# Two mixture-of-experts layers: the first experts' rows from a one-hot product, the overflow loop at the last pair, the memory keys among the output projection

## The chip, the cores and the metric

The kernel runs on one core of one Trainium2 chip. A time is the device time of one execution, in microseconds (us). The kernel before was timed three times: 2768.33, 2773.16 and 2774.87 us, median 2773.16. A further execution was taken with the hardware profiler: 2772.39 us on the device, of which the profile's span (first to last instruction) is 2770.2 us.

The engines are named as in the profile: PE is TensorE (matrix products), PEld its weight loads, DVE is VectorE, ACT is ScalarE, POOL is GpSimd, SP is SyncE, which here issues nearly all DMAs, in order.

## The reference: two mixture layers, then two dense ones

512 tokens of width 1024 pass through two "first blocks" and two "second blocks". A first block is a mixer and then a mixture of experts; a second block is attention, cross attention to a memory of 256 rows, and a dense feed-forward part. What the change touches:

```
for l in range(2):                                   # first blocks
    y = concat(mLSTM, latent attention, spatial gating)(rms_norm(x, attn_norm[l]))
    x = x + y @ w_out[l]
    xt = rms_norm(x, ffn_norm[l])                    # (512, 1024)
    g  = top1(xt @ w_group[l] + b_group)             # 4 groups
    e  = top2 of the 8 experts of group g            # 32 experts, weights softmaxed
    for each expert: rows = its tokens
        h = silu(xt[rows] @ w1[e]) * (xt[rows] @ w3[e])      # 1024 -> 256
        x[rows] += (h @ w2[e]) * weight                      # 256 -> 1024
for i in range(2):                                   # second blocks
    ...
    k, v = split(rms_norm(mem, mem_kv_g[i]) @ x_wkv[i])      # (256, 2048)
    x = x + cross_attention(x, k, v); ...
```

All products are wanted in float32. The kernel makes most of them from two rounded halves of each operand (`mm3`: high*high, high*low, low*high in fp32r, three passes); the experts' products are plain fp32.

## The kernel before

**The planner.** Every operation is first recorded (`Recorder.add`), then `flush` puts them in order: it prices each (`price`: engine time and, for a DMA, a transfer time in one modelled queue), walks a modelled clock, and on each engine picks among the next 24 ready ones the one with the lowest rank (program place less the length of the path behind it). Tiles come from a heap of 46 buffers of 512 KB and 6 half-size ones. The resulting order per engine is fixed; at run time every engine goes through its own list strictly in order. SP's list is a queue in the same sense: a store that waits for its data holds back the loads behind it.

**f1 (L1397 on)** is a mixer layer. Its last piece, `do_out`, multiplies the four token tiles with `w_out` in two column halves; the second half ends tile by tile in `chain_route` (L1897): transposes of x, the split into high and low, the router's product (L1917), and the normalized rows `xn`, which are stored to DRAM as `xm` (L1923).

**route (L1927)** is a chain of some 110 small DVE operations on the router's result, with one product of counts in its middle; it yields `s.sl` (each token's slot) and `s.ovi` (how many blocks of 64 rows do not fit the fixed capacity of 64 rows per expert).

**mem_kv (L1002)** makes the memory's keys and values for the second block `l`: normalize 256 rows, transpose, 8 key chunks (192 products of 256 columns), 4 value tiles (96 products of 512 columns), all stored to DRAM. It stands in the program behind `route`.

**overflow (L2062)** is a hardware loop over `ovi[0]` blocks. With these inputs the count is zero in both layers: no instruction of its body shows in the trace. The loop is recorded as one operation on all engines ("ALL"): each engine reads the count, stops until every engine has come and the DMAs issued are done, and goes on. It stands before the experts.

**moe (L2163 on)** runs 16 pairs of experts. `prep_group` builds one-hot matrices and from them the row numbers of four pairs; `prep_pair` gathers a pair's 128 rows from DRAM with an indirect DMA on POOL's queue and transposes them (8 transposes); `up` is 32 products of 256 columns in fp32 (two experts side by side in the array's columns; the profile shows 64 records), `down` 8 products of 512, `combine` adds two pairs back to the tokens with 32 products of 512. Each pair's weights are 12 loads of 512 KB (`raw<-w`), 192 loads per layer.

```
G.memset(x, 0.0)                    # two gather buffers, L2171 on
prep_group(0); prep_pair(0)
for p in range(NP + 1):
    up(p, w13)
    prep_pair(p + 1)                # gather, then transposes
    down(p - 1); combine every second pair
```

In `run` (L2287 on) a layer is `f1`, `route`, `mem_kv`, the loads of two pairs, `overflow`, `moe`.

Of the kernel before, what the change touches and what calls it, by code (L numbers as in the profile page):

```python
# [85 lines left out]
class Recorder:  # L86
# [127 lines left out]
    @staticmethod  # L214
    def price(eng, method, outs, ins, k):

        def free(x):
            n = 1
            for v in x.shape[1:]:
                n *= int(v)  # L220
            return n
        if eng == "ALL":
            return 2500, 0
        n = max(free(x) for x in outs + ins) if method != "matmul" else free(outs[0])
        if eng == "PE":
# [6 lines left out]
        psum = any(x.tensor.space == PSUM for x in ins)  # L232
        if eng == "SP" or "dma" in method:
# [241 lines left out]
class Kern:  # L475
# [526 lines left out]
    def mem_kv(s, i):  # L1002

        nc = s.nc
        W = s.I["x_wkv_2"][i]
        kd = s.dr.tile([D, 256], F32, name=f"memk{i}")
        vd = s.dr.tile([256, D], F32, name=f"memv{i}")
        g = s.gain(s.I["mem_kv_g_2"][i])
        mT = s.newXT(256)
        for t in range(2):  # L1010
            m = s.H(name="mem")
            nc.sync.dma_start(m, s.I["mem_2"][0, t * 128:(t + 1) * 128, :])
            xn = s.norm(m, g)
            s.to_T(t, xn, mT)
        for cb in range(2):
            def ck(c, ps):
                o = s.T2()
                nc.scalar.copy(o[:, 0:256], ps[:, 0:256])
                r = (cb * 4 + c) * 128
                nc.sync.dma_start(kd[r:r + 128, :], o[:, 0:256])  # L1020
            s.lin_T(mT, 8, W, cb * 512, 128, 4, ck)
        for cb in range(2):
            w = s.wload(W, 0, 8, D + cb * 512, 512)
            for t in range(2):
                ps = s.PS()
                for k in range(8):
                    s.mm3(ps, mT.get(k, t * 128, t * 128 + 128), w[k], k == 0, k == 7)
                o = s.T2()
                nc.scalar.copy(o, ps)
                nc.sync.dma_start(vd[t * 128:(t + 1) * 128, cb * 512:(cb + 1) * 512], o)  # L1030
        return kd, vd

    def cross(s, i, act, kv, nxt):
        nc = s.nc
# [359 lines left out]
                        streams.remove(x)  # L1394
                        break

    def f1(s, l, act, nxt, xsrc):  # L1397
        nc, I = s.nc, s.I
        xT = act.xT
        W = I["w_in"][l]  # L1400
# [164 lines left out]
        def do_mla():  # L1565
            yield from s.mla(b1, done, doneh)
# [3 lines left out]
        def do_out():  # L1570
            tail = None
            for hf in range(2):
# [3 lines left out]
                for t in range(NT):  # L1576
# [24 lines left out]
                        A.copy(y, ps)  # L1601
                    yield

        def seq(*fs):
# [292 lines left out]
    def chain_route(s, l):  # L1897

        c = Chain(None, None)

        def prep():
            s.moe_start(l)
            s.rg = s.gain(s.I["ffn_norm"][l])

        def f(t):
            nc = s.nc
            if c.act is None:
                c.act = s.newXT()
            xT, x = c.act, s.x[t]
            s.to_T(t, x, xT)  # L1910
            r, v, xn = s.SM(1, "rt_r"), s.SM(1, "rt_v"), s.H(name="xn")
            s.stat(x, r, v)
            ps = s.PS()
            for k in range(8):
                hl = xT.get(k, t * 128, t * 128 + 128)
# [7 lines left out]
            nc.sync.dma_start(s.xm[t * 128:(t + 1) * 128, :], xn)  # L1923
        c.prep, c.call = prep, f
        return c

# [236 lines left out]
    def moe(s, l, raws, nxt):  # L2163
# [4 lines left out]
        mm = nc.tensor.matmul  # L2168
        xe, info, w2, us = {}, {}, {}, {}
        s.nc.AGE = 1000  # L2170
        xring = [s.H(name="xg") for _ in range(2)]  # L2171
        for x in xring:
            G.memset(x, 0.0)
        xring = s.ring(xring, D)
        NP = 16

        def prep_group(g):
            slg = s.SM(8, "slg", 2)
# [11 lines left out]
                    mm(ps[:, pr * 6:(pr + 1) * 6], P[k][:, pr * 128:(pr + 1) * 128], s.rec[:, k * 6:(k + 1) * 6], start=k == 0, stop=k == 7)  # L2190
            info[g] = s.slots(ps[:, 0:24], 4, 128, "sl")

        def prep_pair(p):
            g, i = divmod(p, 4)
            xg = xring()
            s.gather(nc, s.xm, xg, info[g][3][:, i:i + 1])
            x = s.H(name="xe")
            for a in range(2):
                tp = s.TP()
# [67 lines left out]

        if isinstance(nxt, Chain):
            nxt.prep()
        prep_group(0)  # L2270
        prep_pair(0)
        for p in range(NP + 1):
            if p < NP:
                w13, w2[p] = raws.pop(0) if raws else s.pair_raw(l, p)
                up(p, w13)
            if p + 1 < NP:
                prep_pair(p + 1)
                if p % 4 == 1 and p < 12:
# [8 lines left out]
    def run(s):  # L2287
# [40 lines left out]
```

## Time and profile before

| | us or share |
|---|---|
| profiled execution | 2772.39 |
| its span | 2770.2 |
| PE busy | 2675.2 (97%) |
| PEld busy | 2150.9 (78%) |
| DVE busy | 1523.6 (55%) |
| ACT busy | 1169.9 (42%) |
| POOL busy | 632.6 (23%) |
| DMA moved | 421.92 MB |

In the trace the first layer's experts run from about 346 to 615 us, the second layer's from about 948 to 1216. [...] A "record" is one line of the trace; an fp32 product has two of them. In the view by windows a row reads: the stretch, its length, then busy us and instructions of PE, PEld, DVE, ACT and POOL, PE's clock, the DMA engines' busy share, GB/s. In a timeline: start, us, engine, line, operation, tile written and tiles read, size, instructions, in brackets the idle time before and what ended it. In the waits view a row reads: engine, tile and line that waited, what it waited for, us in total, number of waits, the longest.

### The profile page before, as it was taken

What the parts mean: (1) busy time and instruction counts of PE and PEld (TensorE: products, weight loads), DVE (VectorE), ACT (ScalarE), POOL (GpSimd) and SP (SyncE); (2) the same over time, 40 slices, a digit from 0 to 9 for tenths busy, and PEclk for the clock granted to TensorE, in tenths of its full rate; (3) what the DMA queues carried; (4) which work ended last, traced back from release to release, by engine and by line L of the source; (5) the groups of instructions that cost most, each with busy time, mean ns of one, the idle gap of its engine ahead of it and who ended that gap; (6) DMA issues with size and microseconds to landing.
All of it is one profiled execution on the core that took longest, in us unless ns stands there. A gap on an engine that the chain in (4) does not pass through costs nothing.

```text
span 2770.2 us, 40611 instructions
## 1 busy us (share of the span) xinstructions
PE 2675.2 (97%) x15112; PEld 2150.9 (78%) x15112; DVE 1523.6 (55%) x3275; ACT 1169.9 (42%) x2406; POOL 632.6 (23%) x752
## 2 busy tenths in 40 slices
PE   8999799999999899999999999999999999999998
PEld 7878756559888666568788988888888879888887
DVE  6696534346796344363689553344548885542433
ACT  5555211125555011154697442233346764432331
POOL 1613100003523000012454111001325541110012
PEclk9999899999999999999999999999999999999999
DMA  6124899962135999940124322233311233322321
GB/s 178 30 77 161 307 406 370 401 204 81 37 104 198 352 392 389 391 151 28 37 68 145 99 92 73 88 107 106 111 59 51 65 125 101 95 80 78 116 91 47
DMA packets 224056, 421.92 MB, mean 152 GB/s; under 512 B 46064, under 2 KB 112368, under 8 KB 223856
## 3 DMA queue, kind: packets, MB, share of 16 engines
q1 hardware_dynamic: 219248, 410.89, 42.7%
q0 software_dynamic: 4608, 8.40, 0.8%
q8 instruction: 121, 1.98, 0.3%
q14 instruction: 79, 0.65, 0.1%
HBM read 410.83 MB, written 16.78 MB: 154 GB/s over the span
## 4 chain that ended last, share of the span: by engine, by line
PE 81%; DVE 8%; ACT 3%; DMA 3%; issue 3%; POOL 1%; SPq 0%; POOLq 0%; DVEq 0%; ACTq 0%
PE mm L385 75%; PE tp L385 6%; DVE wl L385 2%; DMA xg<-xm,slidx 2%; DVE t L385 1%; ACT t L385 1%; DVE x L385 1%; DMA raw<-w 1%; ACT wh L385 1%; ACT qh L385 0%; DVE nm L385 0%; DMA raw<-x_wkv 0%; DVE xtl L385 0%; DVE pt L385 0%; SPq L385 0%
## 5 line engine op out<-in xcount | busy, mean ns | idle before, releaser
L385 PE MATMUL mm<-wh,xth 128*128 128x512 f32 (+3 forms) x1088 | 403.5, 396 | 0.5 <-ACT xth L385 0.5
L385 PE MATMUL mm<-wl,xth 128*128 128x512 f32 (+3 forms) x1088 | 400.7, 393 | 1.1 <-DVE wl L385 1.0
L385 PE MATMUL mm<-wh,xtl 128*128 128x512 f32 (+3 forms) x1088 | 400.9, 393 | 0.2 <-DVE xtl L385 0.2
L385 DVE SCALAR_TENSOR_TENSOR wl<-raw,pre_g,wh 128x512 fp32r<-128x512 f32 (+4 forms) x400 | 286.3, 755 | 151.6 <-ACT wh L385 121.5
L385 PE MATMUL mm<-xth,wh 128*128 128x512 f32 (+1 forms) x1184 | 364.8, 359 | 0.1
L385 PE MATMUL mm<-xth,wl 128*128 128x512 f32 (+1 forms) x1184 | 364.5, 358 | 0.0
L385 PE MATMUL mm<-xtl,wh 128*128 128x512 f32 (+1 forms) x1184 | 363.4, 357 | 0.0
L385 ACT ACTIVATE wh<-raw,pre_g 128x512 fp32r<-128x512 f32 (+4 forms) x400 | 252.0, 685 | 67.9 <-DMA raw<-w_gate_up 50.8
L385 PEld LDWEIGHTS mm<-xtl,wh 128*128 128x128 f32 x1184 | 219.7, 190 | 31.1
L385 PEld LDWEIGHTS mm<-xth,wl 128*128 128x128 f32 x1184 | 219.4, 190 | 30.9
L385 PEld LDWEIGHTS mm<-xth,wh 128*128 128x128 f32 x1184 | 219.2, 190 | 31.1 <-ACT xth L385 0.3
L385 PE MATMUL mm<-raw,xe 128*64 128x256 f32 x2048 | 234.8, 385 | 0.0
L385 PEld LDWEIGHTS mm<-wl,xth 128*128 128x128 f32 x1088 | 204.5, 189 | 35.0 <-DVE wl L385 2.4
L385 PEld LDWEIGHTS mm<-wh,xth 128*128 128x128 f32 x1088 | 204.1, 188 | 35.3 <-ACT xth L385 2.2
L385 PEld LDWEIGHTS mm<-wh,xtl 128*128 128x128 f32 x1088 | 204.8, 188 | 33.6 <-DVE xtl L385 0.7
L385 PEld LDWEIGHTS mm<-raw,xe 128*64 128x64 f32 x2048 | 145.1, 138 | 84.4 <-issue 11.0
L385 POOL TENSOR_TENSOR ffl<-t,ffh 128x512 fp32r<-128x512 f32 x44 | 60.3, 1371 | 544.0 <-ACT ffh L385 506.3
L385 DVE TENSOR_TENSOR wl<-raw,wh 128x1024 fp32r<-128x1024 f32 x112 | 142.1, 1274 | 48.3 <-ACT wh L385 41.2
L385 ACT CAST wh<-raw 128x1024 fp32r<-128x1024 f32 (+2 forms) x128 | 120.4, 956 | 35.1 <-DMA raw<-w_down 30.7
L385 PE MATMUL mm<-raw,t 128*64 128x512 f32 x512 | 125.1, 634 | 7.0 <-ACT t L385 6.9
L385 PE MATMUL mm<-wh,ffh 128*128 128x512 f32 x352 | 130.1, 389 | 0.0
L385 PE MATMUL mm<-wh,ffl 128*128 128x512 f32 x352 | 129.1, 390 | 0.0
(338 smaller groups left out, 4822.6 us busy)
## 6 DMA issues: line engine op xcount, KB each, us to landing
raw<-w SPq DMA_DIRECT2D x384, 512.0 KB, 9.5
raw<-w_gate_up SPq DMA_DIRECT2D x176, 256.0 KB, 3.3
raw<-w_down SPq DMA_DIRECT2D x40, 512.0 KB, 3.8
raw<-x_wkv SPq DMA_DIRECT2D x32, 512.0 KB, 7.3
raw<-a_w_in SPq DMA_DIRECT2D x24, 512.0 KB, 4.0
raw<-b_w_in SPq DMA_DIRECT2D x24, 512.0 KB, 4.1
raw<-w_in SPq DMA_DIRECT2D x24, 384.0 KB, 3.3
raw<-w_out SPq DMA_DIRECT2D x16, 512.0 KB, 3.9
```

Of the source, the lines that this page charges most:

```text
L385: r = o.fn(*o.a, **o.k)
```

## The change

Five edits:

1. **Keys among the mixer.** `mem_kv` now returns two functions. `keys` (normalization, transposes, 8 key chunks) becomes a fifth stream of `f1`, started once five of the eight head results are done; `values` runs after `route`.
2. **Router in smaller tiles.** `chain_route` holds the transposed x per token tile (`TokXT`), so the four splits of 256 columns per engine and tile become two of 512. The tiles `xn` are kept in SBUF.
3. **First pair by a product.** `first_pair` builds, per token tile, the one-hot of slots 0 to 127 (two DVE operations of 128 columns) and multiplies it with `xn`: 32 fp32 products with 128 columns, whose stationary side takes every eighth column of `xn`. Pair 0 has no gather and no transposes any more. Gathers of later pairs are issued two pairs ahead (`fetch`) into three buffers in place of two.
4. **Overflow at the last pair.** The loop is recorded when the last pair's loads have been and before its `up`.
5. **Prices.** A DMA is planned at 400 or 310 (by contiguous bytes) in place of 360, an indirect DMA's delay at 4500 ns in place of 1710; groups are prepared one pair earlier.

```diff
-            return (1040, 1710) if eng == "POOL" else (475, 1100), int(b.shape[0]) * free(b) * DSIZE[b.dtype] / 360
+            return (1040, 4500 if "indirect" in method else 1710) if eng == "POOL" else (475, 1100), int(b.shape[0]) * free(b) * DSIZE[b.dtype] / s_rate(outs + ins)
...
+        def do_beside():
+            while len(doneh) < 5:
+                yield
+            yield from beside()
+
-        s.merge(seq(do_b1, do_csg)); s.merge(seq(do_prep), seq(do_v, do_mo, do_q, do_k, do_mlstm), do_mla(), do_out())
+        s.merge(seq(do_b1, do_csg)); s.merge(seq(do_prep), seq(do_v, do_mo, do_q, do_k, do_mlstm), do_mla(), do_out(), do_beside())
...
-                c.act = s.newXT()
+                c.act = TokXT()
             xT, x = c.act, s.x[t]
-            s.to_T(t, x, xT)
+            xT.add(s)
+            for q in range(2):
+                tp = s.TP()
+                for i in range(4):
+                    nc.tensor.transpose(tp[:, i * 128:(i + 1) * 128], x[:, (4 * q + i) * 128:(4 * q + i + 1) * 128], s.ident)
+                s.split(tp, xT.h[t][:, q * 512:(q + 1) * 512], xT.l[t][:, q * 512:(q + 1) * 512])
...
+        def first_pair():
+
+            oh = s.T2()
+            for t in range(NT):
+                o = oh[:, t * 128:(t + 1) * 128]
+                V.tensor_scalar(o, s.iota[:, 0:128], s.sl[:, t * 2:t * 2 + 1], None, op0=ALU.is_equal)
+                V.scalar_tensor_tensor(o, s.iota[:, 0:128], s.sl[:, t * 2 + 1:t * 2 + 2], o, op0=ALU.is_equal, op1=ALU.add)
+            x = s.H(name="xe")
+            for a in range(2):
+                ps = s.PS()
+                for j in range(4):
+                    for t in range(NT):
+                        mm(ps[:, j * 128:(j + 1) * 128], s.xn[t][:, a * 4 + j:D:8], oh[:, t * 128:(t + 1) * 128], start=t == 0, stop=t == NT - 1)
+                (A.copy if a else V.tensor_copy)(x[:, a * 512:(a + 1) * 512], ps)
+            xe[0] = x
...
+        first_pair()
+        xring = [s.H(name="xg") for _ in range(3)]
...
         prep_group(0)
-        prep_pair(0)
+        fetch(1)
         for p in range(NP + 1):
             if p < NP:
                 w13, w2[p] = raws.pop(0) if raws else s.pair_raw(l, p)
+                if p == NP - 1:
+                    s.overflow(l)
                 up(p, w13)
+            if p + 2 < NP:
+                fetch(p + 2)
...
-            s.f1(l, c.act, s.chain_route(l), I["x"][0] if l == 0 else s.xd)
+            m, keys, values = s.mem_kv(l)
+            kv.append(m)
+            s.f1(l, c.act, s.chain_route(l), I["x"][0] if l == 0 else s.xd, keys)
             s.route()
-            kv.append(s.mem_kv(l))
+            values()
             raws = [s.pair_raw(l, p) for p in range(2)]
-            s.overflow(l)
```

How the order moves at three places of the first layer. (Every recorded operation has the recorder's line, L385 before and L395 now.)

PE before, from the end of the overflow loop on: the last two products of `prep_group` (`tp<-rt_rec,P`), the transposes of gathered rows (`tp<-const,xg`), the first pairs' `up` (`mm<-raw,xe`).

```order
L2076 REGISTER_ALU
L2076 COMPARE_AND_BRANCH
L2076 UNCONDITIONAL_BRANCH
L385 LDWEIGHTS P
L385 MATMUL tp<-rt_rec,P 128x6
...
L385 MATMUL tp<-const,xg 128x128 x13
L385 MATMUL mm<-raw,xe 64x256 x16
```

PE now, up to the first `up`: `mm<-t,xn` is the one-hot product, the rows with 512 columns are the memory's values.

```order
L395 MATMUL tp<-t_717,const 128x32 x14
...
L395 MATMUL mm<-t_781,xn 128x128 x4
...
L395 MATMUL mm<-t_781,xn 128x128 x26
L395 MATMUL mm<-wh,xth 128x512
L395 MATMUL mm<-wl,xth 128x512 x2
...
L395 MATMUL mm<-wl,xth 128x512
L395 MATMUL mm<-raw,xe 64x256 x32
```

The loop is gone from in front of the experts, nothing gathered is used by pair 0, and 96 value products that all stood ahead of the loop are now spread: 16 ahead of the one-hot product and within its start, 14 between it and the first `up`, the rest behind that, 32 of them ahead of the first transposes of gathered rows.

PE before at the last two pairs: `tp<-const,t` and `mm<-raw,t` are a pair's `down`.

```order
L385 MATMUL tp<-const,t_1189 128x128 x2
L385 MATMUL mm<-raw,t_1189 64x512 x8
L385 MATMUL mm<-raw,xe 64x256 x32
L385 MATMUL tp<-const,t_1220 128x128 x2
L385 MATMUL mm<-raw,t_1220 64x512 x8
L385 MATMUL mm<-yh,pT 128x512
```

And now:

```order
L395 MATMUL tp<-const,t_1173 128x128 x2
L395 MATMUL mm<-raw,t_1173 64x512 x8
L395 MATMUL mm<-raw,xe 64x256 x19
L2105 TENSOR_LOAD rt_ovi
L2106 COMPARE_AND_BRANCH
L2106 UNCONDITIONAL_BRANCH x2
...
L2106 REGISTER_ALU
...
L395 MATMUL mm<-raw,xe 64x256 x13
L395 MATMUL tp<-const,t_1222 128x128 x2
L395 MATMUL mm<-raw,t_1222 64x512 x8
```

The loop's stop now stands inside the last pair's `up`, after 19 of its 32 products (after 27 in the second layer).

SP before, in front of the loop and behind it: `memk` and `memv` are stores of keys and values, `raw<-w` experts' weights, `raw<-w_in` the next layer's.

```order
L385 DMA raw<-w 128x1024 x11
L385 DMA memk_665<-t_719 128x256
...
L385 DMA memv_666<-t_753 128x512
L2075 TENSOR_LOAD rt_ovi
...
L385 DMA memv_666<-t_755 128x512
L2076 COMPARE_AND_BRANCH
...
L385 DMA raw<-w 128x1024 x168
L385 DMA raw<-w_in 128x2x416
```

And now:

```order
L395 DMA raw<-w 128x1024 x7
L2105 TENSOR_LOAD rt_ovi
...
L395 DMA memv_117<-t_737 128x512
L395 DMA raw<-w 128x1024 x5
L395 DMA memv_117<-t_739 128x512
...
L395 DMA memv_117<-t_755 128x512
L395 DMA raw<-w 128x1024 x153
L395 DMA raw<-w_in 128x2x416
...
L2106 COMPARE_AND_BRANCH
```

The loads of weights are no longer cut by the loop; the four stores of values now stand among the 24th to 40th load, and of the next layer's weights one load stands ahead of the loop (three in the second layer) where all eight and more did.

## Rows read from the trace of the kernel before

**Rows 1.** By windows: layer 0's router, layer 0's experts, layer 1's router.
```profile
262.00:278.30 16.30, 13.80 (x96) 12.17 (x96) 13.69 (x24) 12.42 (x23) 6.94 (x5) 1.00 0.88 293
...
361.40:480.00 118.60, 117.97 (x864) 73.26 (x863) 52.47 (x113) 22.01 (x41) 9.29 (x10) 1.00 0.99 385
...
868.70:884.70 16.00, 13.51 (x94) 11.92 (x94) 13.34 (x24) 12.13 (x23) 6.62 (x5) 1.00 0.88 298
```
**Rows 2.** Waits of PE from 330 to 350, layer 0.
```profile
PE tp L385 <- DMA xg<-xm,slidx: 7.4, 1, 7.4
PE tp L385 <- issue: 7.0, 1, 7.0
```
**Rows 3.** Waits of PE from 936 to 960, layer 1.
```profile
PE tp L385 <- DMA xg<-xm,slidx: 6.9, 1, 6.9
PE tp L385 <- issue: 4.3, 1, 4.3
```
**Rows 4.** Timeline at the loop, layer 0.
```profile
329.01 1.46 POOL L385 DMA_INDIRECT xg<-xm,slidx  x1 [12.49 <-DVE P L385]
...
336.57 0.21 PE L385 MATMUL tp<-rt_rec,P 128*128 128x6 bf16 x2 [6.96 <-issue]
...
345.95 1.33 PE L385 MATMUL tp<-const,xg 128*128 128x128 f32 x5 [7.36 <-DMA xg<-xm,slidx]
```
**Rows 5.** Chain of work that ended last: start, us, what.
```profile
276.88 19.84 PE mm L385 x164
...
347.28 5.50 PE mm L385 x32
...
361.46 3.60 PE mm L385 x32
...
949.03 5.01 PE mm L385 x32
```
**Rows 6.** Timeline of PE: four fp32 products of 128 columns; eight transposes of gathered rows.
```profile
219.04 1.05 PE L385 MATMUL mm<-qkm 96*128 96x128 f32 x8
...
502.75 1.13 PE L385 MATMUL tp<-const,xg 128*128 128x128 f32 x8
```
**Rows 7.** Weight loads, 20 to 640: count, busy us, mean ns, idle.
```profile
L385 PEld LDWEIGHTS tp<-const,xg 128*128 128x128 f32 x128 | 16.8, 196 | 13.9 <-DMA xg<-xm,slidx 7.8 <-issue 4.0 <-PE mm L385 1.3
...
L385 PEld LDWEIGHTS tp<-const,x 128*128 128x128 f32 x64 | 8.1, 140 | 3.2 <-DVE x L385 1.8
```
**Rows 8.** Timeline of DVE in the routing, layer 0.
```profile
279.83 1.80 DVE L385 TENSOR_TENSOR rt<-rt 128x16 f32<-128x16 f32 x1
...
281.84 1.22 DVE L385 TENSOR_TENSOR wl<-raw,wh 128x1024 fp32r<-128x1024 f32 x1
...
295.68 0.29 DVE L385 TENSOR_TENSOR t<-t 128x128 f32<-128x128 f32 x1
```
**Rows 9.** Timeline of PE at the end of layer 0's experts.
```profile
571.85 0.51 PE L385 MATMUL tp<-const,t 128*128 128x128 f32 x2 [1.48 <-DMA raw<-w]
572.82 5.35 PE L385 MATMUL mm<-raw,t 128*64 128x512 f32 x16 [0.46 <-ACT t L385]
...
594.04 3.65 PE L385 MATMUL mm<-raw,t 128*64 128x512 f32 x16 [0.46 <-ACT t L385]
```
**Rows 10.** Gathers, 320 to 640: time from issue to landing.
```profile
DMA to landing us min/median/max: 6.5/7.6/9.6
```
**Rows 11.** Timeline of SP's queue, layer 0.
```profile
318.00 11.93 SPq L385 DMA_DIRECT2D memv<-t  x4
336.16 231.13 SPq L385 DMA_DIRECT2D raw<-w  x168
568.69 0.38 SPq L385 DMA_DIRECT2D raw<-w_in  x1
```
**Rows 12.** DVE, 560 to 640: splits of the next layer's first weights.
```profile
L385 DVE SCALAR_TENSOR_TENSOR wl<-raw,pre_g,wh 128x416 fp32r<-128x416 f32 x8 | 4.9, 645 | 1.6 <-ACT wh L385 1.6
```
**Rows 13.** Waits of PE, whole span.
```profile
PE tp L385 <- DMA raw<-w: 1.9, 3, 1.5
```

More of the change, by code (lines that the diff above doesn't have):

```diff
@@ L232, in price, with s_rate @@
         psum = any(x.tensor.space == PSUM for x in ins)
+        def s_rate(aps):
+            x = next(v for v in aps if v.tensor.space == bass.MemoryType.DRAM)
+            n = 1
+            for st, c in reversed(list(x.ap)):
+                if st != n and c > 1:
+                    break
+                n *= c
+            return 400 if n * 4 >= 2048 else 310
         if eng == "SP" or "dma" in method:
             b = outs[0] if outs[0].tensor.space != bass.MemoryType.DRAM else ins[0]
-            return (1040, 1710) if eng == "POOL" else (475, 1100), int(b.shape[0]) * free(b) * DSIZE[b.dtype] / 360
+            return (1040, 4500 if "indirect" in method else 1710) if eng == "POOL" else (475, 1100), int(b.shape[0]) * free(b) * DSIZE[b.dtype] / s_rate(outs + ins)
         small = sum(isinstance(x, bass.AP) for x in (k.get("scale"), k.get("bias"), k.get("accum_out")))
@@ L1007, in mem_kv, with keys, ck, values @@
         vd = s.dr.tile([256, D], F32, name=f"memv{i}")
[L1008 to L1023, printed above, removed]
-            for t in range(2):
[L1025 to L1031, printed above, removed]
+        made = []
+        def keys():
+            g = s.gain(s.I["mem_kv_g_2"][i])
+            mT = s.newXT(256)
+            made.append(mT)
+            for t in range(2):
+                m = s.H(name="mem")
+                nc.sync.dma_start(m, s.I["mem_2"][0, t * 128:(t + 1) * 128, :])
+                xn = s.norm(m, g)
+                s.to_T(t, xn, mT)
+                yield
+            for cb in range(2):
+                def ck(c, ps):
+                    o = s.T2()
+                    nc.scalar.copy(o[:, 0:256], ps[:, 0:256])
+                    r = (cb * 4 + c) * 128
+                    nc.sync.dma_start(kd[r:r + 128, :], o[:, 0:256])
+                yield from s.lin_T_steps(mT, 8, W, cb * 512, 128, 4, ck)
+        def values():
+            mT = made[0]
+            for cb in range(2):
+                w = s.wload(W, 0, 8, D + cb * 512, 512)
+                for t in range(2):
+                    ps = s.PS()
+                    for k in range(8):
+                        s.mm3(ps, mT.get(k, t * 128, t * 128 + 128), w[k], k == 0, k == 7)
+                    o = s.T2()
+                    nc.scalar.copy(o, ps)
+                    nc.sync.dma_start(vd[t * 128:(t + 1) * 128, cb * 512:(cb + 1) * 512], o)
+        return (kd, vd), keys, values
     def cross(s, i, act, kv, nxt):
@@ L1395, in merge, with f1 @@
                         break
-    def f1(s, l, act, nxt, xsrc):
+    def f1(s, l, act, nxt, xsrc, beside):
         nc, I = s.nc, s.I
@@ L1602, in do_out @@
                     yield
+        def do_beside():
+            while len(doneh) < 5:
+                yield
+            yield from beside()
         def seq(*fs):
@@ L1902, in prep @@
             s.moe_start(l)
+            s.xn = []
             s.rg = s.gain(s.I["ffn_norm"][l])
@@ L1923, in f @@
             nc.sync.dma_start(s.xm[t * 128:(t + 1) * 128, :], xn)
+            s.xn.append(xn)
         c.prep, c.call = prep, f
@@ L2170, in moe @@
         s.nc.AGE = 1000
[L2171 to L2174, printed above, removed]
         NP = 16
+        xgs = {}
         def prep_group(g):
@@ L2191, in prep_group, with fetch @@
             info[g] = s.slots(ps[:, 0:24], 4, 128, "sl")
+        def first_pair():
[6 more added lines that the diff above has]
+            for a in range(2):
+                ps = s.PS()
+                for j in range(4):
[3 more added lines that the diff above has]
+            xe[0] = x
+        def fetch(p):
+            g, i = divmod(p, 4)
+            xgs[p] = xring()
+            s.gather(nc, s.xm, xgs[p], info[g][3][:, i:i + 1])
         def prep_pair(p):
-            g, i = divmod(p, 4)
-            xg = xring()
-            s.gather(nc, s.xm, xg, info[g][3][:, i:i + 1])
+            xg = xgs.pop(p)
             x = s.H(name="xe")
@@ L2269, in moe @@
             nxt.prep()
+        first_pair()
+        xring = [s.H(name="xg") for _ in range(3)]
+        for x in xring:
+            G.memset(x, 0.0)
+        xring = s.ring(xring, D)
         prep_group(0)
-        prep_pair(0)
+        fetch(1)
         for p in range(NP + 1):
@@ L2274, in moe @@
                 w13, w2[p] = raws.pop(0) if raws else s.pair_raw(l, p)
+                if p == NP - 1:
+                    s.overflow(l)
                 up(p, w13)
+            if p + 2 < NP:
+                fetch(p + 2)
             if p + 1 < NP:
                 prep_pair(p + 1)
-                if p % 4 == 1 and p < 12:
+                if p % 4 == 0 and p < 12:
                     prep_group(p // 4 + 1)
```

## The prediction

> **What bounds the kernel now.** I read first how busy each engine is by stretches, then PE's waits in the two stretches where it is not full, then the timeline around them, and last the queue that feeds the experts. The reader is to see this. In the middle of the first layer's experts PE is busy 117.97 of 118.60 us at full clock, and the DMA engines are busy 0.99 of the time: two resources are nearly full together [rows 1]. PE is the one that leads: in the whole program it waits only 1.9 us for a weight [rows 13], and the 168 loads behind the loop need 231.13 us, so the last is away at 567.3 while PE works on pairs 14 and 15 [rows 9, 11]. So what counts is PE's idle time and PE's own work. Idle time at the start of the experts: 7.0 + 7.4 us in layer 0 [rows 2], 4.3 + 6.9 us in layer 1 [rows 3]. The first of the two is the loop: the gather of pair 0 is issued at 329.01, it takes at least 6.5 us to land [rows 10], that is to 335.5, and PE goes on at 336.57 [rows 4], about 1.1 us later; no engine passes the loop with a gather on its way. The second is the gather of pair 1, whose transposes stand in front of pair 0's `up` on PE: PE stands 7.36 us and goes on at 345.95 [rows 4]. In the routers PE idles 2.5 us each (16.30 less 13.80, 16.00 less 13.51) [rows 1].
>
> **What is removed (layer 0 / layer 1).**
> (a) The two waits, 14.4 / 11.2 us [rows 2, 3]: with the loop gone from there and pair 0 made by a product, neither has a place.
> (b) The slow clock behind them. After these pauses the first 32 records of `up` take 5.50 and 5.01 us, where they take 3.60 later [rows 5]; that is 1.9 / 1.4, and I add 0.6 for transposes of which five took 1.33 us [rows 4] where eight take 1.13 [rows 6]. 2.5 / 2.0.
> (c) The routers' 2.5 us of idle time each fall to about 1.0, since keys and two splits of 512 in place of four of 256 fill or shorten it: 1.6 / 1.6. Bounds 0 and 2.5.
> Sum 18.5 / 14.8.
>
> **What is added.**
> (d) The first pair: 32 fp32 products of 128 columns. Four of these (8 records) took 1.05 us with the pipe's run-out [rows 6]; 32 are at most 8.4. Without the run-out the floor is near that of a pair's 64 `up` records, 7.2 (twice 3.60) [rows 5]. I take 7.5. The eight transposes of pair 0 go, 1.13 [rows 6]: net 6.4 in each layer. The upper bound comes from the stationary side. It takes every eighth column, as the transposes of gathered rows do, and such a weight load took 196 ns against 140 for whole columns [rows 7]; 64 loads of 196 are 12.5 if they set the pace, net 11.4. Against that speaks that eight such transposes still took 1.13 us, 0.14 each, so these loads ran beside the products [rows 6].
> [...]
> (e) New waits in front of the experts, where `values` alone is left as cover. The routing chain on DVE ran from 279.83 to 295.97, but eight splits of the key weights up to 1.22 long stood in it [rows 8]; without them some 6.3 to 7 us. Behind the last router product there are now 62 key products of 0.121 us (164 in 19.84 [rows 5]) and three of values, about twice that each: 8.2 in all. Hidden but for the delay with which the counts' product comes: 0.8. Behind it, the one-hots with 13 value products (3.1 us) as cover: 1.0. Then pair 1's gather: issue 1.46 [rows 4] and half a us for its row numbers, landing 7.6 [rows 10], 9.6, against 32 value products (7.7) and some 1.0 of `prep_group` products: 0.9. Sum 2.7 in each layer, bounds 0 (all is covered) and 6 (nothing is late but each link is doubled). Of pair 0's rows only SBUF tiles are used, so its stores to DRAM delay nothing but the gather of pair 1. The stores of values now stand among the 24th to 40th load on SP and hold the later ones until they are computed; with two pairs of weights loaded PE reaches the third a pair and a half later, so I price this at nothing.
> (f) The loop in the last pair. No gather is under way there, so it drains quickly: the 1.1 us from above plus half a us for the small loads, 1.6; bounds 1.1 and 7.0 [rows 2, 4]. Behind a pause of 1.48 us the next `down` took 5.35 in place of 3.65 us [rows 9]: 1.7 more. 3.3 in each layer.
> (g) In layer 0 one of the pauses between the last `up` products and their `down` (1.48 + 0.46 [rows 9]) is now filled by a combination: −1.9 / 0.
> (h) Queued behind the loop is the next layer's work: on SP all but one load of its first weights (three in layer 1), which started at 568.69 before [rows 11], and on DVE and ACT their splits; eight take 4.9 us on DVE [rows 12]. PE still has 13 (5) products, a `down` and the last combinations to do, which hide most. I take 1.0 each; bounds 0 and 4.9.
> Sum 11.5 / 13.4.
>
> Everything else, the new prices' order of loads included, I put at nothing: in the middle of the experts PE idles 0.6 of 118.6 us [rows 1], so there is nothing to win there, and the weights keep their lead.
> Together: 33.3 less 24.9 is 8.4 us. The profiled execution took 2772.4 us (2.2 more than its span, which I leave as it is) and is 0.8 below the median of the three runs, too little to correct for: 2764.
>
> **The rivals.**
> Strided loads set the pace: 12.5 in place of 7.5 us for the first pair, 10 us more in both layers, 2774, no change. For it rows 7, against it rows 6.
> The late loop costs as much as the early one (slower): it drains 7.0 us [rows 2] in place of 1.6 since loads of the next layer are just under way, and the whole 4.9 of splits [rows 12] then stands in front of the next mixer in place of 1.0. That is 9.3 in each layer, 18.6 in all, 2782.6. It decides from 7.0 us more in each layer (8.4 + 5.5 over two). For it: PE waited 7.0 for whatever was on its way. Against it: no gather is on its way now.
> The DMA engines set the pace after all: then what the loop cost is the pause of the weight stream from 318.00 to 336.16 [rows 11], 18.2 us, and it comes back whole in each layer, 36.4 less the new loop's 6.6: 2742.6. For it: 0.99 busy in the experts [rows 1]. [...] Against it: 1.9 us of waits for weights [rows 13], and a last load some 30 us ahead of its `down`.
>
> **Chances.** Forecast 0.50 (2755 to 2770 by its own bounds), strided loads 0.16, the late loop 0.18, DMA 0.16. A measurement tells a change from none at about 0.2%, 5.5 us. Faster: 0.40 of the forecast's 0.50 and the DMA's 0.16, 0.56. Same: the forecast's other 0.10, 0.12 of the strided loads, 0.02 of the late loop: 0.24. Slower: 0.04 and 0.16, 0.20. The range 2745 to 2782 leaves out the far half of the DMA case and about half of the late loop's.
>
> **What would show it.** (a) No wait of PE for `xg` or "issue" in front of the experts, and (b) the first `up` records at 3.60. (c) Router stretches with about 1 us idle. (d) `mm<-t,xn` summing to 7.2 to 8.4 us, not 12. (e) PE waiting for the counts or `oh` 1 us each, not 3. (f) A pause of PE of 1 to 2 us within the last `up`. (h) The first products of the next mixer waiting for `wl` or `wh` at most 1 us more. The forecast is wrong if PE waits for `raw<-w` early in the experts, or if the second layer's waits are not removed as the first's are.

## The result, and the profile after

The changed kernel takes 2807.59 us, median of four runs (2798.51 to 2809.4), against 2772.29 before: slower, by a ratio of 1.0122, 95% interval [1.0097, 1.0147]. The forecast was 2764 and the range ended at 2782. The profiled execution is the fastest of the four (2798.51, span 2796.7, clock 0.989 where the others show 0.985 to 0.987; a clock is PE's granted one, as a share of its full one), so the traces account for 26 of the 35 us. PE is busy 2705.3 us now, 30 more than before; its idle time in the span is 91, where it was 95. In the traces the loss lies wholly in the two mixture layers: the first ends its last `down` at 623.6 us in place of 612.4, the second 615.9 us after that in place of 599.9, and the rest takes 1557 us in place of 1558.

What the change was to remove is mostly gone. PE's waits over the whole span (engine, tile, line, what it waited for: us, count, longest):

```profile
PE tp L395 <- DVE t L395: 12.0, 10, 2.2
...
PE tp L395 <- DMA xg<-xm,slidx: 6.2, 2, 3.4
PE mm L395 <- ACT t L395: 5.9, 12, 1.1
PE mm L395 <- DVE wl L395: 5.6, 5, 2.1
...
PE tp L395 <- POOL sgo L395: 3.9, 4, 1.5
...
PE mm L395 <- issue: 2.1, 1, 2.1
```

In front of the experts PE stood 14.4 and 11.2 us [rows 2, 3]; of that one wait for gathered rows a layer is left, 6.2 us in all, and it stands behind the first `up` now. The late loop stops PE 2.1 us in layer 0 ("mm <- issue"). New are waits inside the mixer (`sgo` here, `qkm` below). The waits for `t` from DVE and ACT are the largest that the fence shows, 17.9 us together; they are the pauses in the experts' later pairs. They are not new, only left over: the kernel before has nearly the same two.

```profile
PE tp L385 <- DVE t L385: 10.0, 13, 1.5
PE mm L385 <- ACT t L385: 6.9, 15, 0.5
```

So of PE's idle time some 25 us went in front of the experts, and came back as 11 us in the mixers and 10 in the experts (the late gather and the loop). Its busy time rose by 30, and the one new group of products alone is 30.7 in both layers.

The new PE work is that group. Here it is in layer 0, the weight loads first, then the products (count, busy us, mean ns, idle):

```profile
L395 PEld LDWEIGHTS mm<-t,xn 128*128 128x128 f32 x64 | 15.5, 334 | 0.1
```
```profile
L395 PE MATMUL mm<-t,xn 128*128 128x128 f32 x64 | 15.4, 396 | 0.0
```

Loads and products are busy for the same time, 0.24 us a record. Each load takes 334 ns, so one load overlaps the next: 64 of them end to end would be 21.4 us. A strided load of a transpose took 196 ns [rows 7]. That the loads set the pace is shown by the first experiment below (7.6 us of products with loads of 192 ns).

The first `up` behind it runs at full clock (1.00 from 342.8 to 350.2 us), 64 records in 7.13 us, where the first 32 alone took 5.50 [rows 5], at a clock of 0.65 (timeline of PE: start, us):

```profile
343.07 7.13 PE L395 MATMUL mm<-raw,xe 128*64 128x256 f32 x64
```

The mixer of layer 0, from the transposes of `b` on, by windows (length; busy of PE, PEld, DVE, ACT, POOL; clock; DMA; GB/s). Before, its first part and its output projection with the router:

```profile
128.72:200.17 71.45, 69.34 (x400) 57.15 (x400) 64.93 (x159) 33.14 (x80) 11.66 (x13) 0.95 0.23 68
200.17:296.56 96.39, 93.89 (x615) 82.90 (x615) 69.87 (x164) 54.55 (x103) 32.15 (x25) 1.00 0.56 189
```

And after, between the same instructions:

```profile
130.72:203.83 73.11, 68.10 (x368) 56.87 (x367) 65.40 (x155) 37.34 (x87) 11.72 (x13) 0.91 0.25 85
203.83:315.74 111.91, 106.53 (x689) 93.29 (x690) 69.27 (x158) 50.42 (x91) 31.12 (x25) 0.98 0.47 154
```

The second stretch holds all 192 key products now, where 153 stood in it before, so its length doesn't compare; PE's idle time does (length less busy, both stretches together): 4.6 us before, 10.4 after, with a lower clock in both stretches (0.91 and 0.98, where it was 0.95 and 1.00). DVE is busy 91% of the first one in the kernel before already; that is where the keys' norm and splits were added.

The end of layer 1's experts (timeline of PE, in brackets the pause before and what ended it):

```profile
1160.98 0.50 PE L395 MATMUL tp<-const,t 128*128 128x128 f32 x2 [1.42 <-DVE t L395]
1161.94 5.35 PE L395 MATMUL mm<-raw,t 128*64 128x512 f32 x16 [0.46 <-ACT t L395]
...
1195.24 0.47 PE L395 MATMUL tp<-const,t 128*128 128x128 f32 x2 [1.56 <-DVE t L395]
...
1229.14 1.51 PE L395 MATMUL mm<-raw,xe 128*64 128x256 f32 x10 [2.10 <-DVE wl L395]
1232.86 0.51 PE L395 MATMUL tp<-const,t 128*128 128x128 f32 x2 [2.20 <-DVE t L395]
1234.44 5.11 PE L395 MATMUL mm<-raw,t 128*64 128x512 f32 x16 [1.07 <-ACT t L395]
```

At these three places a pair's `down` stands right behind its own `up`, and PE waits for DVE and ACT to make `t` (1.42 and 0.46 us, 1.56 and 0.46, 2.20 and 1.07). The `down` behind them runs at a lower granted clock (0.68, 0.68 and 0.71) and takes 5.35, 5.35 and 5.11 us in place of 3.65 [rows 9]. The pause of 2.10 at 1229 is the loop; the waiter's label names what came last. The clock did not fall behind every such pause: in layer 0 it was 1.00 behind one of 1.56 us (the last line is that layer's loop and the `up` behind it, at 0.65):

```profile
582.18 0.48 PE L395 MATMUL tp<-const,t 128*128 128x128 f32 x2 [1.56 <-DVE t L395]
583.12 3.65 PE L395 MATMUL mm<-raw,t 128*64 128x512 f32 x16 [0.46 <-ACT t L395]
...
612.71 4.92 PE L395 MATMUL mm<-raw,xe 128*64 128x256 f32 x26 [2.14 <-issue]
```

By windows, the `down` at 583 and one of layer 1 behind the same pause of 1.56 us; the last number but two is the granted clock, 1.00 and 0.68:

```profile
583.12:586.77 3.65, 3.65 (x17) 1.13 (x17) 0.75 (x1) 0.69 (x1) 0.00 (x0) 1.00 0.89 349
```
```profile
1196.17:1201.52 5.35, 5.35 (x17) 1.53 (x17) 0.75 (x1) 0.69 (x1) 0.00 (x0) 0.68 1.01 385
```

### The profile page after: what moved, and what is told of

It is laid out like the page before. It is cut to its first block, busy times and chain, and to the rows that moved or that the text cites. A ratio compares the mean times of both kernels' runs of the same rounds, so it can differ in the third digit from the quotient of the medians.

```text
span 2796.7 us, 40841 instructions
## 1 busy us (share of the span) xinstructions
PE 2705.3 (97%) x15224; PEld 2181.2 (78%) x15224; DVE 1524.0 (54%) x3275; ACT 1166.3 (42%) x2390; POOL 628.7 (22%) x752
## 4 chain that ended last, share of the span: by engine, by line
PE 46%; DVE 5%; ACT 2%; POOL 1%; issue 1%; DMA 0%; DVEq 0%; ACTq 0%; POOLq 0%
PE mm L395 44%; PE tp L395 2%; DVE wl L395 1%; DVE x L395 1%; DVE nm L395 0%; ACT qh L395 0%; DVE pt L395 0%; ACT pring L395 0%; ACT t L395 0%; DVE t L395 0%; DVE y L395 0%; POOL t L395 0%; DMA raw<-x_wq 0%; DVE xnm L395 0%; DVE n_r L395 0%
## 5 line engine op out<-in xcount | busy, mean ns | idle before, releaser
L395 PE MATMUL mm<-wh,xth 128*128 128x512 f32 (+3 forms) x1088 | 405.8, 397 | 2.0 <-DVE hn_r L395 0.8
L395 PE MATMUL mm<-wl,xth 128*128 128x512 f32 (+3 forms) x1088 | 403.8, 393 | 3.8 <-DVE wl L395 3.5
L395 PE MATMUL mm<-wh,xtl 128*128 128x512 f32 (+3 forms) x1088 | 403.0, 393 | 0.2 <-DVE xtl L395 0.2
L395 PE MATMUL mm<-xth,wh 128*128 128x512 f32 (+1 forms) x1184 | 372.4, 359 | 0.8 <-ACT xth L395 0.7
L395 DVE SCALAR_TENSOR_TENSOR wl<-raw,pre_g,wh 128x512 fp32r<-128x512 f32 (+4 forms) x400 | 289.2, 761 | 153.7 <-ACT wh L395 123.2
L395 PE MATMUL mm<-xth,wl 128*128 128x512 f32 (+1 forms) x1184 | 372.5, 359 | 0.0
L395 PE MATMUL mm<-xtl,wh 128*128 128x512 f32 (+1 forms) x1184 | 370.9, 358 | 0.0
L395 ACT ACTIVATE wh<-raw,pre_g 128x512 fp32r<-128x512 f32 (+4 forms) x400 | 252.7, 685 | 78.8 <-DMA raw<-w_gate_up 45.1
L395 PEld LDWEIGHTS mm<-xth,wh 128*128 128x128 f32 x1184 | 222.1, 189 | 32.2 <-ACT xth L395 1.5
L395 PEld LDWEIGHTS mm<-xth,wl 128*128 128x128 f32 x1184 | 222.2, 189 | 30.8
L395 PEld LDWEIGHTS mm<-xtl,wh 128*128 128x128 f32 x1184 | 222.1, 189 | 30.8
L395 PE MATMUL mm<-raw,xe 128*64 128x256 f32 x2048 | 235.7, 384 | 4.2 <-issue 2.1
L395 PEld LDWEIGHTS mm<-wl,xth 128*128 128x128 f32 x1088 | 205.7, 190 | 39.2 <-DVE wl L395 6.4
L395 PEld LDWEIGHTS mm<-wh,xth 128*128 128x128 f32 x1088 | 206.2, 190 | 36.2 <-ACT xth L395 1.7
L395 PEld LDWEIGHTS mm<-wh,xtl 128*128 128x128 f32 x1088 | 205.9, 190 | 34.0 <-DVE xtl L395 0.9
L395 PEld LDWEIGHTS mm<-raw,xe 128*64 128x64 f32 x2048 | 145.1, 138 | 91.2 <-issue 19.2
L395 POOL TENSOR_TENSOR ffl<-t,ffh 128x512 fp32r<-128x512 f32 x44 | 59.4, 1352 | 543.9 <-ACT ffh L395 516.7
L395 DVE TENSOR_TENSOR wl<-raw,wh 128x1024 fp32r<-128x1024 f32 x112 | 140.8, 1263 | 52.5 <-ACT wh L395 42.7
L395 ACT CAST wh<-raw 128x1024 fp32r<-128x1024 f32 (+2 forms) x128 | 121.4, 957 | 54.5 <-DMA raw<-w_down 32.2
L395 ACT ACTIVATE t<-mm 128x256 f32<-128x256 f32 (+3 forms) x72 | 28.7, 402 | 247.8 <-PE mm L395 138.3
L395 PE MATMUL mm<-wh,ffh 128*128 128x512 f32 x352 | 130.2, 390 | 0.0
L395 PE MATMUL mm<-wh,ffl 128*128 128x512 f32 x352 | 129.2, 390 | 0.0
```

The lines of the kernel that those rows point to most:

```text
L395: r = o.fn(*o.a, **o.k)
```

## The experiments

Each kernel was timed 4 to 12 times, with the kernel before timed beside it (medians 2770.8 to 2772.0). Behind each time stands the ratio to that kernel, with its 95% interval; the changed kernel's is 1.0122. "Less" and "more" are against the changed kernel's 2807.59 where nothing else is named.

**Contiguous stationary side.**

```diff
-nc.scalar.activation(xn, x, AF.Copy, scale=r)
+nc.scalar.activation(xn.rearrange("p (j q) -> p q j", j=8), x.rearrange("p (q j) -> p q j", j=8), AF.Copy, scale=r)
-nc.gpsimd.tensor_mul(xn, xn, s.rg)
+xv = xn.rearrange("p (j q) -> p j q", j=8)
+nc.gpsimd.tensor_mul(xv, xv, s.rg.rearrange("p (q j) -> p j q", j=8))
...
-mm(..., s.xn[t][:, a * 4 + j:D:8], oh[...])
+mm(..., s.xn[t][:, (a * 4 + j) * 128:(a * 4 + j + 1) * 128], oh[...])
```

> Rows are written to xn and to DRAM with their columns in the order the products read them, so that the stationary side of the one-hot products (and of the transposes of gathered rows) is 128 whole columns; nothing else moves. Theory (strided loads): a layer's 64 records of the one-hot product fall from 14.6 us to 7 to 8.4 us, their weight loads from 334 ns to about 200 ns, and the time falls by some 14 us, 2807 to 2793. Rival (fp32 products of 128 columns cost that whatever they read): 14.6 us stay, the time stays at 2807.

2795.96 us, 1.0090 [1.0077, 1.0103], 12 less. The same two groups, loads, then products:

```profile
L395 PEld LDWEIGHTS mm<-t,xn 128*128 128x128 f32 x64 | 7.6, 192 | 0.3
```
```profile
L395 PE MATMUL mm<-t,xn 128*128 128x128 f32 x64 | 7.6, 275 | 0.0
```

Half of each, with the order of PE's instructions the same throughout: the stride is what made the product cost 15.4 us, and 7.6 is what the forecast had. Of the 15.6 us saved in both layers 12 come back. Part of the price moves to who writes the columns apart: ACT's copy into `xn` rises from 1152 to 2151 ns and POOL's product from 2404 to 3084, four of each in the router's stretch, and the last router product of layer 0 ends at 309.5 us in place of 306.8. That this is all of the difference is not shown.

**Keys behind the routing.**

```diff
-            s.f1(..., keys)
+            s.f1(..., lambda: iter(()))
             s.route()
+            for _ in keys():
+                pass
             values()
```

> The memory's keys are made behind the routing again and not among the mixer; all else as in the changed kernel. Theory (the fifth stream costs the mixer its order): the mixer from its b transposes to the last router product loses its 4.5 us of extra idle time and the 5 us of slow clock a layer, and the keys cover the routing chain better: 12 to 20 us less, 2787 to 2795. Rival (the new prices reorder the mixer, not the keys): the mixer stays as it is, within 4 us of 2807.

2779.73, 1.0035 [1.0022, 1.0048], 28 less, more than expected. In the traces (21 less) layer 0 reaches its first `up` at 331.3 us in place of 343.1, and layer 1 its own 320.7 us behind layer 0's last `down` in place of 327.6. PE's waits from 165 to 275 us, after and here:

```profile
PE mm L395 <- DVE qkm L395: 1.8, 2, 1.2
PE tp L395 <- POOL sgo L395: 1.5, 1, 1.5
PE tp L395 <- POOL b L395: 1.2, 1, 1.2
```
```profile
PE mm L395 <- DVE apt L395: 1.2, 1, 1.2
PE mm L395 <- DVE mtmp L395: 0.4, 1, 0.4
PE mm L395 <- DVE qkm L395: 0.2, 1, 0.2
```

The mixer's waits go with the keys: the fifth stream was the cause, not the prices, which are unchanged here (and the run with the old prices, below, is no faster: 2807.54).

**No one-hot product.**

```diff
-        first_pair()
...
         prep_group(0)
+        fetch(0)
         fetch(1)
+        prep_pair(0)
```

> Pair 0 is gathered and transposed as before, with two gathers in flight; the loop stays at the last pair. Theory (the one-hot product is the costliest term): 13.5 us less PE work a layer against a gather wait of some 7 us a layer that returns: 10 to 15 us less, 2792 to 2797. Rival (the product pays by hiding the gather): the wait is over 13 us a layer, no gain or a loss, 2807 or more.

2767.94, 0.9986 [0.9976, 0.9996], 40 less: far more than expected. In the traces it is 30, about what the product took (30.7, less the 16 transposes that return, 0.14 us each [rows 6]). The gather it was to replace makes PE wait 1.2 us in layer 0 (from 290 to 380 us) and not at all in layer 1:

```profile
PE tp L395 <- DMA xg<-xm,slidx: 1.2, 1, 1.2
```

With the loop gone from in front, the products of the memory's values stand there and cover the gather. The one-hot product hid next to nothing; it was added to a path on which hardly a wait was left, and for pair 1's gather, which came behind it, PE waited 2.9 us in layer 0.

**Prices of before.**

```diff
-(1040, 4500 if "indirect" in method else 1710)   ... / s_rate(outs + ins)
+(1040, 1710)   ... / 360
```

> The planner's prices of DMAs are those of before; all edits to the program stay. Theory (prices matter little): within 4 us of 2807. Rival (prices reorder the mixer, and that is what the mixer lost): the mixer's extra idle time of 4.5 us a layer and its slow clock go, 10 to 20 us less, 2787 to 2797.

2807.54, 1.0131 [1.0116, 1.0145]: no difference in time, though the written order of PE does differ.

**Late loop alone, in the kernel before.**

```diff
-            s.overflow(l)
...
+                if p == NP - 1:
+                    s.overflow(l)
                 up(p, w13)
```

> The kernel before with one edit: the overflow loop at the last pair. Theory (the loop in front was the cost, by stopping with a gather on its way and by keeping the second gather from being covered by the values' products): PE's 25.6 us of waits in front of the experts and 4.5 us of slow clock behind them nearly go, two stops of some 3 us come: 15 to 23 us less than before, 2748 to 2756. Rival (the gather is late anyway, and a product was needed to replace it): the wait for the gathered rows keeps 7 us or more a layer, 2765 or more.

2752.19, 0.9935 [0.9921, 0.9948], within the theory's range. Of the waits in front this is left (290 to 380 us):

```profile
PE tp L385 <- DMA xg<-xm,slidx: 0.7, 1, 0.7
PE mm L385 <- ACT t L385: 0.5, 1, 0.5
PE mm L385 <- DVE xe L385: 0.3, 1, 0.3
```

So terms (a) and (b) of the forecast hold, and one edit of the five is enough to earn them.

**Both taken back, then the router's tiles too.** Edits as above; the third is `TokXT()` to `s.newXT()` with `s.to_T(t, x, xT)`.

> The changed kernel without the one-hot product and with the keys behind the routing; late loop, smaller router tiles, gathers two pairs ahead and new prices stay. Theory (the two costs add): 40 and 28 us less than 2808, 2740, or by the traces alone 30 and 21 less than 2798, 2747. Rival (keys behind the routing only helped by covering what the one-hot product waits for): no more than 6 us below the run without the product, 2762 or more.

> The kernel of the run before this with the router's tiles undone as well (four splits of 256 columns). Theory (the smaller tiles only shorten a wait of 1 to 2 us a router): 2 to 4 us more than without this edit. Rival (they do nothing that PE sees): within 2 us.

2754.12, 0.9936 [0.9922, 0.9950]; and 2752.05, 0.9926 [0.9912, 0.9939]. What remains of the change without product and keys is as fast as the late loop alone; the router's tiles make no difference that shows. The first was expected at 2740 or 2747: the costs overlap. Keys cost 28 us beside the product and 14 without it; the product 40 beside the keys and 26 without.

**Loop in front, in the changed kernel.**

```diff
             raws = [s.pair_raw(l, p) for p in range(2)]
+            s.overflow(l)
...
-                if p == NP - 1:
-                    s.overflow(l)
```

> The changed kernel with the loop in front of the experts again; the one-hot product, the keys among the mixer and the rest stay. Theory (the loop's place pays): PE stops 4 to 7 us in front of the experts in each layer, against 2 to 4 at the last pair, and less is there to cover pair 1's gather: 4 to 14 us more, 2812 to 2822. Rival (with no gather on its way the stop costs the same anywhere): within 3 us of 2808.

2777.39, 1.0024 [1.0015, 1.0033]: 30 less, where the theory said more and the rival no difference. The loop's place is worth 19 us one way in the kernel before and 30 the other way here. The stop isn't it: in front of layer 0's experts no wait of PE is longer than 1.8 us here (from 290 to 380 us), and the late stop took 2.1. In the traces (18 less) nearly all of the difference arises in layer 1. PE's waits behind 985 us in layer 1's experts, changed kernel, this one, and the kernel before:

```profile
PE tp L395 <- DVE t L395: 6.4, 4, 2.2
PE mm L395 <- ACT t L395: 3.4, 6, 1.1
PE mm L395 <- DVE wl L395: 2.1, 1, 2.1
```
```profile
PE tp L395 <- DVE t L395: 2.9, 2, 1.4
PE mm L395 <- ACT t L395: 0.9, 2, 0.5
PE tp L395 <- POOL t L395: 0.3, 1, 0.3
```
```profile
PE tp L385 <- DVE t L385: 5.7, 6, 1.5
PE mm L385 <- ACT t L385: 3.2, 7, 0.5
```

The waits for `t` shrink with the loop in front here, but the kernel before has them in full with its loop in front too: the loop's place alone does not decide them.

**Loop right behind the routing.** In the changed kernel without product, with the keys behind the routing and the loop behind them (shown); then in the kernel before, where the loop stands ahead of the keys too.

```diff
             s.route()
             for _ in keys():
                 pass
+            s.overflow(l)
             values()
```

> As the run without product and with the keys behind the routing, but the overflow loop is recorded right behind the routing and the keys, ahead of the values, so that the values' products and the gathers stand behind it. Theory (what the loop costs is the work it keeps apart: at the last pair it takes filler from the last downs, in front of the experts it keeps the cover from the gathers): the experts of each layer fall from 272 to 277 us to 260 to 265, as in the run with the loop in front, and the stretch ahead stays at 201 to 204: 2730 to 2742. Rival (the loop's stop itself is the cost wherever it stands): 2752 or more.

> The kernel before with one edit: the overflow loop recorded right behind the routing, ahead of keys and values. Theory as in the run above: the gather waits go as with the late loop (2752), and the last pair keeps its fillers: 2740 to 2750. Rival (there the loop stops PE until the routing chain is through, with half of the keys not yet made): 2755 or more.

2767.21, 0.9984 [0.9973, 0.9996], and 2782.26, 1.0036 [1.0023, 1.0050]: the theory's times are missed by 25 and more, and both rivals' bounds hold. PE's largest waits from 275 to 380 us, of the first, then of the second:

```profile
PE tp L395 <- DVE P L395: 10.7, 5, 8.4
```
```profile
PE tp L385 <- DVE rt L385: 8.2, 1, 8.2
PE mm L385 <- DMA raw<-w: 5.9, 1, 5.9
```

Here the stop for all engines cuts the cover in two: DVE makes the one-hot matrices `P` only behind it (PE's longest wait for them is 8.4 us in the first), and the weights' queue is held (PE waits 5.9 us for `raw<-w` in the second).

**What is left with the loop in front; the contiguous product with the loop early, and in front.** Edits as above, combined.

> The changed kernel without its product, its keys among the mixer and its late loop: what is left is smaller router tiles, gathers two pairs ahead and new prices. Theory (PE waits in front of the experts for both gathers again, 7 to 14 us a layer): 2755 to 2770. Rival (gathers two pairs ahead and the higher price hide them): 2745 or less.

> The first of these runs with the one-hot product added again, its stationary side contiguous: the product at its best, with the loop early. Theory (with the gathers covered by values the product hides nothing, and its 7.6 us less 1.1 of transposes is pure cost): 10 to 16 us more than without it, 2742 to 2755. Rival (it starts the experts some 8 us earlier and pays): at or below the run without it.

> The changed kernel with contiguous one-hot product, keys behind the routing, and the loop in front. Theory (three costs taken back: 12, 28 and 30 us if they added, but keys and loop act on the same waits): 2740 to 2755. It tells whether the product pays against gathers that PE waits for (2753 without product, same loop): below 2747 it does, above 2759 it doesn't.

2753.14, 0.9926 [0.9907, 0.9945]: the wait for gathered rows in front is 5.9 us in layer 0 and 7.8 in layer 1, and the time is a little below the theory's range. So with the loop in front and neither product nor keys the kernel is as fast as with the late loop (2754.12): what it loses in front it gains in the experts, which take 253.3 and 248.1 us from the first `up` to the last `down`, against 265.2 and 263.3 in the kernel before. The loop's place is worth 19 us, nothing or minus 30, by what stands around it. With the contiguous product and the early loop 2792.07, 1.0072 [1.0058, 1.0086], 25 more than without product, above the 10 to 16 expected: it costs more than its 7.6 us a layer, as PE also stands 11.3 and 9.3 us for its one-hots there. With the contiguous product and the loop in front 2761.07, 0.9960 [0.9946, 0.9974]: the wait for gathered rows falls to 0.4 us in layer 0, and the time is still 8 above the run without product, above the range and past the 2759 named beforehand. In none of the four pairs of runs that differ by the product did the one with it win.

**A higher planned rate.** What differs in the later pairs is the written order. Of the changed kernel, then with the rate at 500, the last pairs of layer 0 (U `up`, T and D a pair's `down`, C combination, X transposes of gathered rows):

```
400:  ... X T D C U16 C U16 C T D U32 T D C U16 C U16 C T D U19 LOOP U13 T D C
500:  ... U32 X T X D T C U32 D U32 X T D T C U3 LOOP U29 D T D C
```

```diff
-        return 400 if n * 4 >= 2048 else 310
+        return 500 if n * 4 >= 2048 else 310
```

> The changed kernel with one number changed: long DMAs are planned at 500 in place of 400. Theory (the planner's modelled weights are late, so it puts a pair's down right behind its own up): the waits for DVE and ACT in the later pairs (layer 1: 9.8 us) fall to 3 us or less in each layer and the slow clock behind them goes; 14 to 28 us less, 2780 to 2794. Rival (the weights do come late): PE waits for raw<-w instead, 2803 or more.

> Without the one-hot product, keys behind the routing, late loop, planned at 500. Theory: the same waits (7 to 10 us a layer) and the clock behind them go, 15 to 25 us less than 2754 at 400: 2729 to 2740. Rival (weights come late): 2750 or more.

> The kernel before with the loop at the last pair and all DMAs planned at 500 in place of 360. Theory: the later pairs' waits go (9 to 10 us a layer and the clock behind them), 12 to 22 us less than 2752: 2730 to 2740. Rival (weights come late): 2750 or more.

2785.38, 1.0053 [1.0040, 1.0067], 22 less than the changed kernel; 2731.26, 0.9859 [0.9843, 0.9875], 23 less than at 400; 2733.38, 0.9864 [0.9850, 0.9878], 19 less than at 360. All three lie in the theory's ranges. Waits of PE behind 985 us in layer 1 of the first:

```profile
PE mm L395 <- issue: 2.1, 1, 2.1
PE mm L395 <- ACT t L395: 1.3, 2, 0.7
```

And a stretch of its experts and the same stretch of the changed kernel, by windows:

```profile
1080.00:1173.00 93.00, 93.00 (x666) 59.01 (x663) 35.56 (x65) 15.67 (x30) 3.95 (x4) 1.00 1.03 407
```
```profile
1080.00:1173.00 93.00, 89.45 (x614) 53.31 (x611) 31.90 (x58) 16.77 (x31) 4.94 (x5) 0.98 1.03 407
```

Same DMA share, same 407 GB/s, PE full in the one and not in the other, and PE waits for no weight at 500: the weights were not late on the chip. That they were late in the planner's model, so that it found nothing better to put behind an `up` than its own `down`, is what the three expectations were made from, and they came true; but no run prints the modelled times. Nor is it shown why a loop in front shortens these waits in the changed kernel and not in the kernel before (8.9 us there). A loop in front together with a rate of 500 was not run. Two versions beat the kernel before by 1.4%: that kernel with the late loop and a rate of 500, and the changed one without product and keys at that rate. Between them there is no difference.

## Why the prediction was wrong

The forecast was a gain of 8 us and the traces show a loss of 26. Two steps failed: the price of the first pair's product in (d), and "everything else at nothing", which left out what the keys cost the mixer.

**(a), (b), (f) held.** The waits in front go (14.4 and 11.2 to 2.9 and 3.4 us), the first `up` runs at full clock, the late stop takes 2.1 us where 1.6 was said (half a us of that, for small loads, was the author's estimate, which no row shows); in layer 0 the 26 records behind it took 4.92 us at a clock of 0.65, 2.0 more than at the pace of 64 in 7.13, where 1.7 was said. The late loop alone gives 19 us. (e) is near: 0.7 us for the routing and 2.9 for the gather in layer 0, where 2.7 was said in all, with half a us for row numbers that was an estimate too.

**(d) was mis-sized.** "I take 7.5": measured 15.4 in layer 0 (30.7 us in both), above even the bound of 12.5. The step that failed is the argument "these loads ran beside the products", taken from eight transposes at 1.13 us [rows 6]. It carried over a load time of 196 ns from transposes to products, where it is 334, and a sign of cover from an instruction of another kind. The bound was worked out wrongly too: it multiplied a load's time by their number, but the loads overlapped, and 64 of 334 ns took 15.5 us and not 21.4. The measured loads are on the dear side: 334 ns strided, 192 whole. The rival "strided loads" named the right mechanism; its 2774 still fell short, since its price was too low and the next points were missing.

**(d) again, its worth.** The forecast credited the end of the gather wait to the change as a whole. Once the loop is gone from in front, the values' products cover the gather (1.2 us of wait without the product), so the product had next to nothing to hide. What each edit earns when the others are already made was not asked. Taking the product out gains 40 us, or 26 with the keys back.

**(c) and "everything else at nothing" failed for the keys.** A credit of 1.6 us a layer was booked for filling the routers' idle time; no cost was booked for merging a fifth stream into the mixer, where DVE was nearly full (91% of the first stretch) and PE waits on it (0.9 us there before, 3.6 after). The credit came: PE's waits in layer 0's last router stretch fell from 2.4 us (262 to 278 us before) to 0.3 (285 to 307 after). It was outweighed: keys cost 14 to 28 us, and PE's idle time in the mixer of layer 0 rose from 4.6 to 10.4. Of their interplay with the product, some 14 us, no run shows how it comes about.

**(g) failed, and the order's cause was not seen.** One pause in layer 0 was to be filled; in the trace two pauses for `t` stand at that layer's end as before (1.56 and 1.38 us, where 1.48 and 1.54 stood). Prices were put at nothing because PE is full in the middle of the experts; the run with old prices agrees for 360 against 400, but 500 is worth 19 to 23 us. It acts in the experts' later pairs, which the prediction looked at only for the pause before one `down`.

**The rivals.** The late loop as slow as the early one is refuted (2.1 us of stop, no long wait for the next layer's splits). DMA setting the pace is refuted as well: with the later pairs in a better order PE is 93.00 of 93.00 us busy at the same GB/s. PE does not wait for `raw<-w` early in the experts.

**Sum.** By medians: the late loop gives 19; the product then costs 26, the keys 14, both together 14 more: 35 us slower, the measured difference. The terms hold for this order of taking the edits back, at a planned rate of 400, and the last is what is left over. The 22 us of the planned rate are not among them: product and keys together cost 54 us at 500 (2731 to 2785) as they cost 53 at 400 (2754 to 2808), and the rate gained 19 to 23 us with and without them, each time with the loop late.

## What to carry to other kernels

When a change has several edits that remove the same wait, price each as if the others were made: the cheapest one may take the gain, and then the rest are nearly pure cost. Take the duration of a new instruction from a row of the same kind with the same access pattern, and if none exists let the upper bound weigh. Where a planner writes the order, its rate for a resource is part of the kernel, and the rate nearest to the chip need not give the best order: 400 is within 2% of the 407 GB/s of the trace, and 500, which no trace here shows, was 19 to 23 us better. Try a few, and look in the trace for PE's pauses and for waits on that resource.

## What the runs showed of the hardware

A strided fp32 weight load was dearer for a product (334 ns, whole columns 192) than for a transpose of the same tile shape (196, whole columns 140 [rows 7]), and at 64 in a row it set PE's pace: 15.4 us in place of 7.6 with the same order of instructions. Moving the stride elsewhere cost too: ACT's copy of 1024 columns took 2151 ns in place of 1152 when it wrote neighbours 128 columns apart, and POOL's product 3084 in place of 2404 when it read its gain every eighth column. And a pause of PE could cost more than itself: behind pauses of 1.4 to 2.2 us a `down` of layer 1 took 5.1 to 5.4 us, at a granted clock of 0.68 to 0.71, in place of 3.65 at 1.00; behind a pause of 1.56 us in layer 0 it took 3.65.
